# Transposes of two key pairs and their products with the values queued behind each other, the later pair first

## The chip, the cores and the metric

The kernel runs on one core of a Trainium2 chip. A core has a matrix engine (TensorE, PE in the profile; its weight loads are shown apart as PEld), a vector engine (VectorE, DVE), a scalar engine (ScalarE, ACT), a general engine (GpSimd, POOL) and a queue engine that issues the transfers here (SyncE, SP). The metric is device time in microseconds. The time before is a median of 3044.38 us over three runs, 3041.36 to 3046.33.

## What is computed

One layer on a sequence of 2048 rows of width 1024, in float32. A normalised input is projected once; the projection feeds three branches (attention with forget gates, a state-space layer, and attention into 256 memory rows), each is gated, projected back and merged, and an output projection with a residual and a norm closes it. The change is in the first branch, 12 heads of width 64:

```python
def block(args):
    qi, Fi, s0 = args
    s = jnp.einsum('bhqd,bhkd->bhqk', qi, kh)
    s = s + Fi[..., None] - F[:, :, None, :]
    qpos = s0 + jnp.arange(Q_BLOCK, dtype=jnp.int32)
    s = jnp.where(key_pos[None, :] <= qpos[:, None], s, NEG)
    p = jax.nn.softmax(s, axis=-1)
    return jnp.einsum('bhqk,bhkd->bhqd', p, vh)
```

The attention is causal: a query sees the keys up to its own position.

## The kernel before

**Precision.** Matmuls run on operands split into a high and a low part (hi, lo). The transposes take plain float32. The values `v` hold 64 high and 64 low columns side by side, and the transposed probabilities hold 256 high and 256 low columns side by side, so one product of 128 x 512 gives the cross terms; they are added up at the end of a block.

**Stages.** First the projections, with the state-space layer, the gated unit and the memory attention woven in; then the attention stage; then what is left of the filling, the merge and the output projection (`merge_out`). For the attention stage the eight PSUM banks are shared out anew: three for scores (`psA`), three for transposes (`psB`), one for the accumulated output (`psC`), one for the filling (`psF`).

**A block.** A block is a head `h` and a group `G` of 256 queries (0 to 7), held as two tiles `P[1]` and `P[0]` of 128 queries each; a group sees 2G+2 tiles of 128 keys, taken as G+1 key pairs `kp`. `fox_scores` computes for each of the two query tiles the scores on PE (L751, L752, pieces of up to 512 keys), adds the forget term and takes the maximum on DVE (L753), the exponential on ACT (L758) and the division on POOL (L762). `fox_pv` (L766) then takes one key pair at a time:

- four transposes of 128 x 128 into one `psB` bank (L783; three at the diagonal, where the first query tile does not see the last key tile);
- a cast of the bank to the high half of a `Pt` tile on ACT (L786), and the remainder into the low half on DVE (L787); at the diagonal in two pieces each (L791, L792). There are three `Pt` buffers;
- two products with the values (L799), which accumulate over all key pairs in the block's one `psC` bank.

Behind the last pair the bank is added up (`ot`, L802 and L803), multiplied by a gate and stored (L805 to L808).

**The order.** `gen_fox` (L810) is a Python generator that runs through the blocks. While the scores of one block are written down, the key pairs of the block before it are taken between them: half of its steps after the first query tile, the rest after the second. A step is what `fox_pv` does up to a `yield`, one key pair. After each `yield` of `gen_fox`, `run` adds 0.355 (`PACE`) to a due count, and whenever that reaches 1 it lets the filling go one step: the rest of the projection of the merge gates (`gen_gl`), then the merge of the last quarter (`gen_merge0`), six matmuls or so a step on `psF`. A step of the filling is queued on PE behind the product that was the last one written down 8 yields earlier (`LAG`, kept in `self.pe` and `marks`).

The order of the text isn't the order of issue. A scheduler goes through the program with simulated durations; on each engine it issues what is ready, by priority, which is the order of the text. An engine's issued order is then fixed, and each engine works through its own in turn. `issue_after(x)` puts the instructions of its block that are on the engine of `x` behind `x`; `high_priority()` lets an instruction go ahead of others that are ready.

The rest of the names: `hd` holds a head's keys, values and forget terms; `po` is the `psC` bank; `load_w` (L134) and `split` (L888) bring weights and split them on POOL (L893) or ACT (L891) and DVE (L895); `mm3` (L144) issues three matmuls for a split product (L147 to L149).

Of the kernel before, what the change touches and what calls it, by code (L numbers as in the profile page):

```python
# [5 lines left out]
F32R = mybir.dt.float32r  # L6
# [39 lines left out]
def fl32(ap):  # L46
    return ap.bitcast(F32)


class Layer:  # L50
# [649 lines left out]
        close()  # L700


    def open_fox(self):
        self.fp, self.close_fp = self.pool("foxh", side="right")
        self.k0, self.q0 = [self.fox_keys(0, 0), self.fox_keys(0, 1)], self.fox_q(0, 3)
# [60 lines left out]
    def fox_pv(self, p, h, hd, G, P):  # L766

        nc, s = self.nc, self.s
        po = self.psC()
        cs = slice(G * 256, (G + 1) * 256)  # L770
        r = slice(h * DH, (h + 1) * DH)
        gf = p.tile([64, 256], F32, tag="gf", name="gf", bufs=2)
        nc.sync.dma_start(out=gf, in_=s["gf"][r, cs])
        for kp in range(G + 1):
            ps = self.psB()
            t = p.tile([128, 2, 512], F32R, tag="Pt", name="Pt", bufs=3)
            hi, lo = t[:, :, 0:256], t[:, :, 256:512]
            for a in range(2):
                kt = 2 * kp + a
                for b in range(2):  # L780
                    if kt <= 2 * G + b:
                        o = a * 256 + b * 128
                        nc.tensor.transpose(ps[:, o:o + 128], P[b][:, kt * 128:(kt + 1) * 128], self.ident)  # L783
            psv = ps.rearrange("p (a n) -> p a n", a=2)
            if kp < G:
                nc.scalar.copy(hi, psv)  # L786
                nc.vector.tensor_sub(lo, psv, fl32(hi))  # L787
            else:
                for a in range(2):
                    c = slice(a * 128, 256)  # L790
                    nc.scalar.copy(hi[:, a, c], psv[:, a, c])  # L791
                    nc.vector.tensor_sub(lo[:, a, c], psv[:, a, c], fl32(hi[:, a, c]))  # L792
            for a in range(2):
                kt = 2 * kp + a
                v = hd[kt // 8][1][:, kt % 8, :]
                o, m = po, t[:, a, :]
                if kt == 2 * G + 1:
                    o, m = (z.rearrange("p (x b n) -> p x b n", x=2, b=2)[:, :, 1, :] for z in (o, m))
                self.pe = nc.tensor.matmul(o, v, m, start=(kt == 0), stop=(kt == 2 * G + 1))  # L799
            yield  # L800
        t = p.tile([128, 256], F32, tag="ot", name="ot", bufs=1)
        nc.scalar.copy(t, po[:, 256:512])  # L802
        nc.vector.tensor_add(t, po[:, 0:256], t)  # L803
        o = p.tile([64, 256], F32, tag="oo", name="oo", bufs=2)
        nc.scalar.copy(o, t[64:128])  # L805
        nc.gpsimd.tensor_add(o, o, t[0:64])
        nc.gpsimd.tensor_mul(o, o, gf)
        nc.sync.dma_start(out=s["yx"][r, cs], in_=o)  # L808
# [352 lines left out]
```

## Time and profile before

| what | value |
| --- | --- |
| median of three runs | 3044.38 us (3041.36 to 3046.33) |
| the profiled execution | 3032.29 us, of it 3030.5 us from the first to the last instruction |
| granted clock of TensorE over the span | 0.992 |
| transposes L783 | 1632 |
| products L799 | 864 |
| casts L786 and L791 | 336 and 192 |
| subtractions L787 and L792 | 336 and 192 |

The profile is one execution of the program. Times are in microseconds from the span's start. Matmuls overlap each other, so the duration that a row gives for one is longer than its distance to the next; distances from start to start tell what it costs in a stream. A row of the waits has who waited, for whom, the sum, the times and the longest. A row of the groups has the line, the engine, the operation, the tiles, the form and the count, then busy time and the mean of one in nanoseconds, then the idle time ahead of them and what ended it. In the timeline and in the chain a row has the start, the length and the instructions, neighbours of one kind merged.

### The profile page before, as it was taken

How to read it: one execution, taken by the hardware profiler on the slowest of the kernel's cores; microseconds unless marked ns; L12 is line 12 of the kernel's file. 1: busy time of each engine (PE TensorE's matmuls, PEld its weight loads, DVE VectorE, ACT ScalarE, POOL GpSimd, SP SyncE). 2: the span in 40 equal slices, each digit the busy share in tenths (PEclk: the TensorE clock that was granted, in tenths of full speed). 3: DMA queues.
4: the chain of work that ended last, by engine and by line, in shares of the span. 5: the costliest groups of instructions: out<-in, count | busy, mean ns of one | idle time of the engine just before them, and what ended most of it. 6: DMA issues, size and time to landing. Idle time of an engine off the chain costs nothing.

```text
span 3030.5 us, 43647 instructions
## 1 busy us (share of the span) xinstructions
PE 2956.7 (98%) x14656; PEld 2424.2 (80%) x14656; DVE 1842.2 (61%) x4982; ACT 1044.1 (34%) x2049; POOL 864.8 (29%) x1160
## 2 busy tenths in 40 slices
PE   9999999999999999999999999999999897999999
PEld 7889977777777778888878888888888786788787
DVE  5333399899896673322216777777777875554444
ACT  5102111111112231222215666666666563332222
POOL 0010000000002342112215665565665662222100
PEclk9999999999999999999999999999999999999999
DMA  5343323323334655344352433444443548776542
GB/s 169 108 126 107 106 87 106 126 87 116 122 130 150 175 167 172 105 135 132 116 167 87 123 116 112 117 119 118 126 119 114 172 123 264 226 244 209 175 146 98
DMA packets 306671, 417.80 MB, mean 138 GB/s; under 512 B 84084, under 2 KB 165236, under 8 KB 306436
## 3 DMA queue, kind: packets, MB, share of 16 engines
q1 hardware_dynamic: 306160, 414.95, 44.9%
q8 instruction: 116, 1.90, 0.3%
q14 instruction: 107, 0.88, 0.1%
q10 hardware_dynamic: 288, 0.07, 0.0%
HBM read 276.00 MB, written 138.90 MB: 137 GB/s over the span
## 4 chain that ended last, share of the span: by engine, by line
PE 80%; DMA 9%; DVE 5%; issue 3%; POOL 2%; ACT 1%; SPq 0%; DVEq 0%; POOLq 0%; ACTq 0%
PE psF L147 10%; PE psF L148 10%; PE psF L149 10%; PE psA L149 8%; PE psA L147 8%; PE psA L148 8%; PE psC L799 6%; PE psB L783 5%; PE psA L752 3%; PE psA L751 3%; PE psC L147 2%; PE psC L149 2%; PE psC L148 2%; DMA wraw<-in_w_out 1%; DMA yr<-s_ys 1%
## 5 line engine op out<-in xcount | busy, mean ns | idle before, releaser
L147 PE MATMUL psF<-hh,whi 128*128 128x512 f32 (+1 forms) x1160 | 468.2, 404 | 5.5 <-DVE elo L228 2.5
L149 PE MATMUL psF<-hh,wlo 128*128 128x512 f32 (+1 forms) x1160 | 459.5, 396 | 0.0
L148 PE MATMUL psF<-hl,whi 128*128 128x512 f32 (+1 forms) x1160 | 459.1, 396 | 0.0
L893 POOL TENSOR_SCALAR whi<-wraw 128x1024 fp32r<-128x1024 f32 (+2 forms) x134 | 137.0, 1023 | 710.3 <-PE psA L148 307.0
L147 PE MATMUL psA<-hh,whi 128*128 128x512 f32 (+1 forms) x816 | 322.6, 397 | 2.5 <-POOL whi L893 1.5
L148 PE MATMUL psA<-hl,whi 128*128 128x512 f32 (+1 forms) x816 | 323.9, 397 | 0.0
L149 PE MATMUL psA<-hh,wlo 128*128 128x512 f32 (+1 forms) x816 | 321.8, 395 | 0.8 <-DVE wlo L895 0.8
L895 DVE TENSOR_TENSOR wlo<-wraw,whi 128x1024 fp32r<-128x1024 f32 (+2 forms) x168 | 204.9, 1221 | 191.8 <-POOL whi L893 152.5
L799 PE MATMUL psC<-Pt,v 128*128 128x512 f32 x864 | 266.1, 398 | 6.8 <-DVE ot L803 3.4
L787 DVE TENSOR_TENSOR Pt<-psB,Pt 128x512 fp32r<-128x512 f32 x336 | 226.4, 686 | 75.7 <-ACT Pt L786 73.2
L147 PEld LDWEIGHTS psF<-hh,whi 128*128 128x128 f32 x1160 | 218.6, 188 | 52.2 <-DVE elo L228 3.2
L149 PEld LDWEIGHTS psF<-hh,wlo 128*128 128x128 f32 x1160 | 218.4, 188 | 51.3 <-DVE wlo L895 0.4
L148 PEld LDWEIGHTS psF<-hl,whi 128*128 128x128 f32 x1160 | 218.7, 189 | 45.7 <-issue 0.4
L753 DVE CUSTOM_DVE_ANT_0 P<-psA,nf 128x512 f32<-128x512 f32 (+1 forms) x336 | 201.3, 627 | 45.7 <-PE psA L752 25.4
L786 ACT CAST Pt<-psB 128x512 fp32r<-128x512 f32 x336 | 191.7, 585 | 97.3 <-PE psB L783 52.4
L762 POOL TENSOR_SCALAR P<-P,rd 128x768 f32<-128x768 f32 (+1 forms) x240 | 192.1, 815 | 61.5 <-DVE rd L759 40.6
L751 PE MATMUL psA<-kk,qh 128*128 128x512 f32 (+1 forms) x480 | 185.1, 391 | 3.4 <-DVE mx L753 1.6
L147 PEld LDWEIGHTS psA<-hh,whi 128*128 128x128 f32 x816 | 154.0, 189 | 38.0 <-POOL whi L893 1.9
L149 PEld LDWEIGHTS psA<-hh,wlo 128*128 128x128 f32 x816 | 154.4, 189 | 35.9 <-DVE wlo L895 1.2
L148 PEld LDWEIGHTS psA<-hl,whi 128*128 128x128 f32 x816 | 154.4, 189 | 33.4
L799 PEld LDWEIGHTS psC<-Pt,v 128*128 128x128 f32 x864 | 153.8, 190 | 33.7 <-DVE Pt L787 5.6
L783 PE MATMUL psB<-ident,P 128*128 128x128 f32 x1200 | 176.3, 273 | 0.3
(373 smaller groups left out, 6243.1 us busy)
## 6 DMA issues: line engine op xcount, KB each, us to landing
wraw<-in_w_in SPq DMA_DIRECT2D x90, 512.0 KB, 4.1
s_gl<-ehi SPq DMA_DIRECT2D x96, 256.0 KB, 2.6
g<-s_gl SPq DMA_DIRECT2D x96, 256.0 KB, 4.6
wraw<-in_w_proj SPq DMA_DIRECT2D x40, 320.0 KB, 4.0
s_vs<-ev_v SPq DMA_DIRECT2D x48, 256.0 KB, 2.7
nf<-s_nf SPq DMA_DIRECT2D x24, 512.0 KB, 6.6
v<-s_vs SPq DMA_DIRECT2D x24, 512.0 KB, 6.1
qh<-s_qh SPq DMA_DIRECT2D x96, 128.0 KB, 3.7
```

Of the source, the lines that this page charges most:

```text
L147: nc.tensor.matmul(out, a[0], b[0], start=first, stop=False)
L148: nc.tensor.matmul(out, a[0], b[1], start=False, stop=False)
L149: nc.tensor.matmul(out, a[1], b[0], start=False, stop=last)
L751: nc.tensor.matmul(ps[:, :wm], q[0][:, qs], kk[:, c0:c0 + wm], start=True, stop=False)
L753: nc.vector.tensor_tensor_reduce(out=pr[:, c * 512:c * 512 + w], in0=ps[:, :w], in1=nf[:, c0:c0 + w], scale=1.0, scalar=-3.0e38, op0=ALU.a ...
L762: nc.gpsimd.tensor_scalar(out=c, in0=c, scalar1=rd, scalar2=0.5, op0=ALU.mult, op1=ALU.mult)
L783: nc.tensor.transpose(ps[:, o:o + 128], P[b][:, kt * 128:(kt + 1) * 128], self.ident)
L786: nc.scalar.copy(hi, psv)
L787: nc.vector.tensor_sub(lo, psv, fl32(hi))
L799: self.pe = nc.tensor.matmul(o, v, m, start=(kt == 0), stop=(kt == 2 * G + 1))
L893: self.nc.gpsimd.tensor_scalar(out=hi, in0=x, scalar1=sc, scalar2=1.0, op0=ALU.mult, op1=ALU.mult)
L895: self.nc.vector.tensor_sub(lo, x, fl32(hi))
```

## The change

`fox_pv` takes two key pairs at a time, `j` and `j + 1` (the last one alone where G+1 is odd). It takes two `psB` banks and two `Pt` tiles, and writes down the transposes of both pairs, the later pair's first. Each transpose but the first is put behind the one before it (`issue_after`) and given high priority, by the new helper `behind`. The casts and subtractions follow, the earlier pair's first. Where there are two pairs, a `yield` stands here. Then come the products, four of them, again the later pair's first and each behind the one before it. Since the order of the accumulation has changed, the flag that starts it goes with the first product written down and the flag that ends it with the last. The number of yields of a block stays at G+1.

```diff
@@ -1,3 +1,5 @@
+from contextlib import contextmanager
+
 import concourse.bass as bass
 import concourse.tile as tile
 from concourse import mybir
@@ -700,6 +702,15 @@
         close()
 
 
+    @contextmanager
+    def behind(self, last):
+
+        if last is None:
+            yield
+        else:
+            with self.tc.issue_after(last.ins), self.tc.high_priority():
+                yield
+
     def open_fox(self):
         self.fp, self.close_fp = self.pool("foxh", side="right")
         self.k0, self.q0 = [self.fox_keys(0, 0), self.fox_keys(0, 1)], self.fox_q(0, 3)
@@ -771,32 +782,45 @@
         r = slice(h * DH, (h + 1) * DH)
         gf = p.tile([64, 256], F32, tag="gf", name="gf", bufs=2)
         nc.sync.dma_start(out=gf, in_=s["gf"][r, cs])
-        for kp in range(G + 1):
-            ps = self.psB()
-            t = p.tile([128, 2, 512], F32R, tag="Pt", name="Pt", bufs=3)
-            hi, lo = t[:, :, 0:256], t[:, :, 256:512]
-            for a in range(2):
-                kt = 2 * kp + a
-                for b in range(2):
-                    if kt <= 2 * G + b:
-                        o = a * 256 + b * 128
-                        nc.tensor.transpose(ps[:, o:o + 128], P[b][:, kt * 128:(kt + 1) * 128], self.ident)
-            psv = ps.rearrange("p (a n) -> p a n", a=2)
-            if kp < G:
-                nc.scalar.copy(hi, psv)
-                nc.vector.tensor_sub(lo, psv, fl32(hi))
-            else:
+        first = True
+        for j in range(0, G + 1, 2):
+            kps = range(j, min(j + 2, G + 1))
+            pss = {kp: self.psB() for kp in kps}
+            ts = {kp: p.tile([128, 2, 512], F32R, tag="Pt", name="Pt", bufs=3) for kp in kps}
+            last = None
+            for kp in reversed(kps):
                 for a in range(2):
-                    c = slice(a * 128, 256)
-                    nc.scalar.copy(hi[:, a, c], psv[:, a, c])
-                    nc.vector.tensor_sub(lo[:, a, c], psv[:, a, c], fl32(hi[:, a, c]))
-            for a in range(2):
-                kt = 2 * kp + a
-                v = hd[kt // 8][1][:, kt % 8, :]
-                o, m = po, t[:, a, :]
-                if kt == 2 * G + 1:
-                    o, m = (z.rearrange("p (x b n) -> p x b n", x=2, b=2)[:, :, 1, :] for z in (o, m))
-                self.pe = nc.tensor.matmul(o, v, m, start=(kt == 0), stop=(kt == 2 * G + 1))
+                    kt = 2 * kp + a
+                    for b in range(2):
+                        if kt <= 2 * G + b:
+                            o = a * 256 + b * 128
+                            with self.behind(last):
+                                last = nc.tensor.transpose(pss[kp][:, o:o + 128], P[b][:, kt * 128:(kt + 1) * 128], self.ident)
+            for kp in kps:
+                t = ts[kp]
+                hi, lo = t[:, :, 0:256], t[:, :, 256:512]
+                psv = pss[kp].rearrange("p (a n) -> p a n", a=2)
+                if kp < G:
+                    nc.scalar.copy(hi, psv)
+                    nc.vector.tensor_sub(lo, psv, fl32(hi))
+                else:
+                    for a in range(2):
+                        c = slice(a * 128, 256)
+                        nc.scalar.copy(hi[:, a, c], psv[:, a, c])
+                        nc.vector.tensor_sub(lo[:, a, c], psv[:, a, c], fl32(hi[:, a, c]))
+            if j + 1 <= G:
+                yield
+            last = None
+            for kp in reversed(kps):
+                for a in range(2):
+                    kt = 2 * kp + a
+                    v = hd[kt // 8][1][:, kt % 8, :]
+                    o, m = po, ts[kp][:, a, :]
+                    if kt == 2 * G + 1:
+                        o, m = (z.rearrange("p (x b n) -> p x b n", x=2, b=2)[:, :, 1, :] for z in (o, m))
+                    with self.behind(last):
+                        self.pe = last = nc.tensor.matmul(o, v, m, start=first, stop=(j + 2 > G and kp == j and a == 1))
+                    first = False
             yield
         t = p.tile([128, 256], F32, tag="ot", name="ot", bufs=1)
         nc.scalar.copy(t, po[:, 256:512])
```

## The prediction

> **What bounds the kernel now.** I read the page first, then the busy times by stretch, then the waits, then the chain and the timeline inside the stage that the change touches.
>
> ```profile
> span 3030.5 us, 43647 instructions
> PE 2956.7 (98%) x14656; PEld 2424.2 (80%) x14656; DVE 1842.2 (61%) x4982; ACT 1044.1 (34%) x2049; POOL 864.8 (29%) x1160
> PE 80%; DMA 9%; DVE 5%; issue 3%; POOL 2%; ACT 1%; SPq 0%; DVEq 0%; POOLq 0%; ACTq 0%
> ```
>
> TensorE (PE) is busy 98% of the span and holds 80% of the chain that ended last. The transposes (L783) and the products with the values (L799) run only in the attention stage, about 1605 to 2520 us. Its stretches (columns: length; busy us and count of PE, PEld, DVE, ACT, POOL; granted clock; DMA share; GB/s):
>
> ```profile
> 1605.00:2520.00 915.00, 898.82 (x4830) 747.67 (x4830) 680.14 (x2023) 575.41 (x1161) 559.71 (x794) 0.99 0.42 123
> 1605.00:2340.00 735.00, 729.15 (x3967) 609.63 (x3967) 538.09 (x1659) 476.49 (x954) 439.96 (x636) 1.00 0.40 115
> 2340.00:2520.00 180.00, 169.66 (x866) 138.03 (x865) 142.05 (x365) 98.92 (x208) 119.75 (x158) 0.97 0.52 154
> ```
>
> In 915.0 us PE stands idle for 16.2 us: 5.9 us in the first 735 us (0.8%), 10.3 us in the last 180 us. DVE is busy 74%, ACT 63%. So the stage has two parts that the change can move: the PE time of the instructions themselves, and these 16.2 us. The waits of PE in the stage that name the edited lines:
>
> ```profile
> PE psC L799 <- DVE ot L803: 3.4, 1, 3.4
> PE psC L799 <- DVE Pt L787: 2.9, 2, 2.6
> PE psC L799 <- DVE Pt L792: 0.2, 1, 0.2
> ACT Pt L786 <- PE psC L799: 39.7, 46, 3.3
> ```
>
> Out of 864 products, 4 made PE wait, for 6.5 us in all. The last row is the other direction: ACT waited 46 times for a product to give back a `Pt` buffer, so the ring of three `Pt` buffers is already used up at times, with PE not suffering from it.
>
> **What the change costs, part by part.**
>
> *Number of instructions.* The same transposes, casts, subtractions and products are issued, the same buffers are declared, and no DMA is added, removed or moved past another: the load of `gf` stays in the first step of a block, the store of `yx` behind the last. A block has G+1 steps before and after, so the pace of the filling work (0.355 of a step for each) is the same. The sum is therefore over order alone. Blocks G = 0 to 7 give 0, 1, 1, 2, 2, 3, 3, 4 groups of two, 16 a head, 192 in 12 heads; 48 single key pairs are left.
>
> *Transposes in longer runs.* A run of 4 becomes a run of 8, or of 7 at the diagonal. Does a change between transposes and other matmuls cost something that a longer run saves? The chain view shows runs of all these lengths as they stand (start, us, what):
>
> ```profile
> 1975.00 0.33 PE psB L783 x3
> 1980.40 0.44 PE psB L783 x4
> 1981.30 0.44 PE psB L783 x4
> 1652.76 0.76 PE psB L783 x7
> 1995.16 0.87 PE psB L783 x8
> 2069.24 1.31 PE psB L783 x12
> ```
>
> 3 take 0.33 us, 4 take 0.44, 7 take 0.76, 8 take 0.87, 12 take 1.31: 0.11 us each at every length. The matmul that follows a run might hide a cost, so I check from start to start in the timeline:
>
> ```profile
> 1901.82 1.55 PE L799 MATMUL psC<-Pt,v 128*128 128x512 f32 x6
> 1903.21 0.60 PE L783 MATMUL psB<-ident,P 128*128 128x128 f32 x4
> 1903.57 0.48 PE L147 MATMUL psF<-hh,whi 128*128 128x512 f32 x1
> 1903.89 0.40 PE L148 MATMUL psF<-hl,whi 128*128 128x512 f32 x1
> ...
> 2154.12 1.04 PE L783 MATMUL psB<-ident,P 128*128 128x128 f32 x8
> 2154.92 0.48 PE L751 MATMUL psA<-kk,qh 128*128 128x512 f32 x1
> 2155.23 0.40 PE L752 MATMUL psA<-kk,ql 128*128 128x512 f32 x1
> ```
>
> Six products start 1901.82 and are replaced at 1903.21, 0.23 us each. From the first of 4 transposes to the second matmul behind them is 1903.89 - 1903.21 = 0.68 us; less one matmul of 0.23 that is 0.45 us. For 8 it is 2155.23 - 2154.12 = 1.11, less 0.23, 0.88 us. Two runs of 4 cost 0.90 or 0.88 us, one of 8 costs 0.88 or 0.87: between nothing and 0.02 us less. The price of a change of kind is zero to within the rounding; over 192 groups that bounds the gain at about 4 us, and by the equal runs of 3 to 12 I take **0**.
>
> *Products in fours.* Products in a run cost 0.23 us each, as single matmuls of the filling do (1903.89 above stands 0.32 behind 1903.57 only because that one follows transposes, and this is in the sum just made). **0**.
>
> *The added wait.* The first product of a group is now the later pair's, and the earlier pair's follow it in order: PE must have both casts and both subtractions before all four are through. Behind a waiting product PE's queue holds the other three, and then filling matmuls and scores; for them wait the casts that need a free `Pt`, and on ACT behind those the exponentials. The rows for one pair:
>
> ```profile
> L787 DVE TENSOR_TENSOR Pt<-psB,Pt 128x512 fp32r<-128x512 f32 x336 | 226.4, 686 | 75.7 <-ACT Pt L786 73.2
> L786 ACT CAST Pt<-psB 128x512 fp32r<-128x512 f32 x336 | 191.7, 585 | 97.3 <-PE psB L783 52.4 <-PE psC L799 39.7 <-DVE mx L753 2.2
> L895 DVE TENSOR_TENSOR wlo<-wraw,whi 128x1024 fp32r<-128x1024 f32 (+2 forms) x42 | 58.8, 1400 | 7.5 <-POOL whi L893 5.1 <-ACT whi L891 2.3
> ```
>
> One cast more and one subtraction more is at most 0.585 + 0.686 = 1.27 us; with no cover at all, 192 x 1.27 = 244 us, the far upper bound. Cover is there: 432 pairs in 915 us give PE 2.12 us of work for a pair, 4.24 for a group. The ring sets the tightest loop: with three `Pt` buffers and two in a group, the next group's second cast starts only when the last group's products are done. Products 4 x 0.23 = 0.93, cast 0.59, subtraction 0.69: 2.2 us of the 4.24, which leaves 2.0 us for what stands ahead on ACT and DVE. The usual neighbour on DVE is shorter than that (1.40 us in the mean for the longest kind). So I keep the three waits on `Pt` that exist and make each longer by one subtraction: 3 x 0.69 = **+2 us**. Below, the wait can only shrink by what is there: 6.5 us, and the cold clock behind it.
>
> *Buffers given back earlier.* The second pair's transposes no longer stand behind the first pair's products, so `P` comes free a step sooner; DVE waited for that, but PE did not, so **0**. In return two of the three `psB` banks are taken at once; the next group's first pair has one bank, its second waits for a subtraction that is due before the products anyway: **0** unless the ring binds.
>
> A rule of the Trainium skill, "TensorE: Matmul & The Clock Gate", Part 4, speaks against longer runs: it says that transposes do not count as TensorE activity for the clock gate in the way matmuls do. What it would do here is priced under the rivals; the stretch to 2340 us ran at a granted clock of 1.00 with runs of 8 and 12 in it, so the trace so far speaks against it.
>
> Sum: 0 + 0 + 2 + 0 = +2 us. The profiled execution took 3032.3 us for its span of 3030.5; the median of the runs is 3044.4 (3041.4 to 3046.3), 0.4% above it. Since what I add is a difference, I put it on the median: **3046 us**.
>
> **The rivals.** A measurement of this kernel can tell about 0.2%, 6 us, from no change.
>
> *Faster: stalls go.* The biggest single stall of a product is the 3.4 us for `ot`, the one accumulator bank handed from block to block. Now the first step of a block holds only transposes, so its first product comes later and `ot` has had time. Idle time of PE is also paid for afterwards:
>
> ```profile
> 2355.24 0.50 PE L147 MATMUL psF<-ymg,whi 128*128 128x512 f32 x1 [2.29 <-POOL ymg L893]
> ...
> 2356.05 0.63 PE L751 MATMUL psA<-kk,qh 128*128 128x512 f32 x1
> 2356.48 0.63 PE L752 MATMUL psA<-kk,ql 128*128 128x512 f32 x1
> ...
> 2358.83 0.63 PE L147 MATMUL psF<-ymg,whi 128*128 128x512 f32 x1
> 2359.25 0.69 PE L783 MATMUL psB<-ident,P 128*128 128x128 f32 x4
> ```
>
> After 2.29 us of idling matmuls stand 0.43 apart instead of 0.23; the timeline shows that from 2356.05 to 2359.25, eight of them, 8 x 0.20 = 1.6 us. All 6.5 us of the products' waits with one such tail give 8 us less: 3036 us. The far bound is all 16.2 us with three tails (5 us): 3023. For it: every wait named is at a point that the change moves. Against it: with 4 waits in 864 the old order was hardly late.
>
> *Slower: the ring of `Pt`.* The 2.0 us of margin are gone when something long stands ahead of a cast or a subtraction. It happens now:
>
> ```profile
> 1865.88 3.07 DVE L895 TENSOR_TENSOR wlo<-wraw,whi 128x1024 fp32r<-128x1024 f32 x1
> ...
> 1869.01 1.26 DVE L787 TENSOR_TENSOR Pt<-psB,Pt 128x512 fp32r<-128x512 f32 x2
> 1869.73 0.73 PE L799 MATMUL psC<-Pt,v 128*128 128x512 f32 x2 [2.56 <-DVE Pt L787]
> ```
>
> A weight subtraction of 3.07 us held two `Pt` subtractions back, and PE stood 2.56 us. There are 42 such subtractions in the stage, and 2 waits of that kind now. If one in four lands in a group without margin, that is 9 stalls more, 9 x 2.56 = 23 us, and 3067 us; with a tail of 1.6 us on half of them, 3074. It decides from three stalls more (8 us). For it: the 46 waits of ACT for `Pt`, with a ring that has now to serve two at a time. Against it: the filling matmuls may run ahead by 8 steps and are there to stand between.
>
> *The order does not become what the text says.* Chained instructions issue behind each other, but others can come between where a bank or an operand is late; then the runs stay short. By the transposes' rows that costs and brings nothing: 3044 us, inside the forecast's range.
>
> *Slower: the clock.* If a run of 8 (0.87 us) let the clock drop as the idle of 2.29 us did, each would cost the 1.6 us above, 192 x 1.6 = 307 us, 3352 us. The run of 12 stands in a stretch at clock 1.00, so this is nearly out. That is what the skill's rule would make of it.
>
> **How the numbers follow.** No change within 0.2% (my forecast, with the order that does not form): 0.42, own range 3038 to 3051. Stalls go: 0.24. The ring: 0.32. The clock: 0.02. Faster 0.24, same 0.42, slower 0.34. For 8 in 10 the range leaves out the deep end of the gain (all idle time gone) and the ring's cost beyond the nine stalls with their tails, and the clock: **3030 to 3076 us**.
>
> **What would show it.** Right: runs of 8 and 7 of L783 at 0.87 and 0.76 us, runs of 4 of L799 at 0.93, PE idle in the stage still near 16 us, clock 1.00 up to the filling's change. The ring: the wait of L799 for `Pt` L787 grows from 2.9 us to over 10, and ACT's wait for L799 well over 39.7. The gain: the row of L799 on `ot` is gone and nothing has come for it. The forecast is wrong in its base if 8 transposes take another time than 0.87 us, or if the end of the attention stage moves against its start by more than PE's idle time does.

## The result, and the profile after

The changed kernel takes 3081.3 us in the median of four runs (3076.9 to 3083.5), the kernel before, run beside it, 3044.7. The ratio is 1.0119, with a 95% interval of 1.0107 to 1.0132: 36.6 us slower, and 5 us above the end of the range. The two profiled executions stand 50.1 us apart (3032.3 and 3082.4); that of before is on the low side of its runs. I use the traces for where the time went and the ratios for how much.

The first and last start of the products with the values show where. From the view of that line, before and after (the first number group is the shortest, middle and longest duration in ns):

```profile
L799 PE MATMUL psC<-Pt,v x864: 274/393/775, 1612.1 to 2513.4; 128*128 128x512 f32 x154, 128*128 128x256 f32 x19
```

```profile
L822 PE MATMUL psC<-Pt,v x864: 274/395/775, 1616.1 to 2566.8; 128*128 128x512 f32 x156, 128*128 128x256 f32 x17
```

901.3 us became 950.7: the attention stage alone grew by 49.4 us, nearly all of the 50.1. What the stage computes is unchanged, so the time is waiting. Three rows of before that are wanted below come first: PE's wait at the scores, and two waits of the casts at the diagonal. Behind them stand the busy times of the changed kernel in the stretch that was quoted of before, and in its whole stage the waits of PE and large ones of all engines:

```profile
PE psA L751 <- DVE mx L753: 1.6, 3, 0.7
ACT Pt L791 <- PE psB L783: 36.7, 40, 2.9
ACT Pt L791 <- DVE Pt L792: 26.9, 31, 3.9
```

```profile
1605.00:2340.00 735.00, 710.86 (x3768) 578.51 (x3766) 510.14 (x1567) 450.35 (x901) 417.12 (x602) 1.00 0.38 109
```

```profile
PE psA L762 <- DVE mx L764: 12.9, 8, 5.6
PE psB L798 <- DVE Pt L805: 9.6, 17, 1.6
...
PE psC L822 <- DVE ot L827: 2.6, 2, 2.2
PE psC L822 <- DVE Pt L805: 2.3, 2, 1.7
```

```profile
POOL nf L750 <- DVE mx L764: 190.1, 76, 9.0
DVE Pt L805 <- ACT Pt L804: 99.6, 122, 4.2
ACT Pt L804 <- PE psB L798: 95.2, 75, 4.8
ACT Pt L809 <- DVE Pt L810: 80.5, 56, 3.2
...
ACT Pt L804 <- PE psC L822: 46.6, 59, 2.1
...
ACT Pt L809 <- PE psB L798: 2.6, 10, 0.9
```

PE idles 24.1 us in the 735 us, where it idled 5.9. Short stalls are not in that number: a matmul's modelled duration of 0.4 us covers a stall of up to 0.16. That matters here. From 1605 us to the end of the stage (2520 us before, 2570 now) PE idles 42.8 us instead of 16.2, which is 26.6 of the 49.4; the rest stands as busy time, 922.2 us instead of 898.8 for the same instructions. The products themselves wait for `Pt` hardly differently, 2.3 us against 2.9 (and 1.0 against 0.2 at the diagonal). What grew is in front of them. The casts of full pairs on ACT (L804) wait for transposes 95.2 us instead of 52.4. The casts at the diagonal (L809) wait for transposes less, 2.6 instead of 36.7, but for subtractions 80.5 instead of 26.9. These are the second pieces of a diagonal tile, which wait for the subtraction of the tile's first piece; this wait on ACT grew most. The subtractions on DVE wait for casts 99.6 instead of 73.2; PE now waits for DVE at the scores (12.9 us, 1.6 before) and at the transposes (9.6 us, none listed before). Each engine works through its queue in the issued order, and the queues have fallen out of step. One group in the changed kernel's timeline shows how:

```profile
2043.91 0.60 PE L798 MATMUL psB<-ident,P 128*128 128x128 f32 x4
...
2047.12 0.60 PE L798 MATMUL psB<-ident,P 128*128 128x128 f32 x4
...
2047.76 0.59 ACT L804 CAST Pt<-psB 128x512 fp32r<-128x512 f32 x1 [2.00 <-PE psB L798]
2048.24 2.01 ACT L769 ACTIVATE P<-P,nm 128x2048 f32<-128x2048 f32 x1
2048.38 0.69 DVE L805 TENSOR_TENSOR Pt<-psB,Pt 128x512 fp32r<-128x512 f32 x1
...
2050.24 0.57 ACT L804 CAST Pt<-psB 128x512 fp32r<-128x512 f32 x1
...
2051.50 0.69 DVE L805 TENSOR_TENSOR Pt<-psB,Pt 128x512 fp32r<-128x512 f32 x1
```

By the issued orders with their buffer numbers, the first four transposes are the later pair's, the next four the earlier pair's, and the two casts are the earlier pair's and then the later one's. So the later pair's bank is full at 2044.5 and nobody empties it. ACT's queue has the earlier pair's cast first, whose transposes come only at 2047.12: ACT idles 2.00 us. The later pair's cast follows at 2050.24 behind an exponential, its subtraction ends at 2052.2, and one of three `psB` banks has been held 8.3 us.

A count in the issued orders: of the transposes in the stage, 237 runs of 4 and 40 of 8 (271 and 19 before); of the products, 147 runs of 4 (48 before). The products did come mostly in fours. Most transposes did not come in eights.

### The profile page after: what moved, and what is told of

It reads as the page before. It is cut to its first block, busy times and chain, and to the rows that moved or that the text cites. A ratio compares the mean times of both kernels' runs of the same rounds, so it can differ in the third digit from the quotient of the medians.

```text
span 3080.6 us, 43423 instructions
## 1 busy us (share of the span) xinstructions
PE 2982.2 (97%) x14656; PEld 2421.8 (79%) x14656; DVE 1842.7 (60%) x4982; ACT 1043.4 (34%) x2049; POOL 864.9 (28%) x1160
## 4 chain that ended last, share of the span: by engine, by line
PE 74%; DMA 11%; DVE 6%; issue 3%; POOL 3%; ACT 2%; SPq 1%; DVEq 0%; POOLq 0%; ACTq 0%
PE psF L149 9%; PE psF L150 9%; PE psF L151 9%; PE psA L151 8%; PE psA L149 8%; PE psA L150 7%; PE psC L822 4%; PE psB L798 4%; PE psA L762 2%; PE psA L763 2%; DMA nf<-s_nf 2%; PE psC L149 2%; PE psC L151 2%; PE psC L150 2%; DMA s_mg<-g 1%
## 5 line engine op out<-in xcount | busy, mean ns | idle before, releaser
L805 DVE TENSOR_TENSOR Pt<-psB,Pt 128x512 fp32r<-128x512 f32 x336 | 225.9, 685 | 100.8 <-ACT Pt L804 99.6
L822 PE MATMUL psC<-Pt,v 128*128 128x512 f32 x864 | 250.6, 400 | 6.7 <-DVE ot L827 2.6
L804 ACT CAST Pt<-psB 128x512 fp32r<-128x512 f32 x336 | 190.0, 585 | 146.1 <-PE psB L798 95.2
L762 PE MATMUL psA<-kk,qh 128*128 128x512 f32 (+1 forms) x480 | 188.3, 395 | 18.1 <-DVE mx L764 12.9
L798 PEld LDWEIGHTS psB<-ident,P 128*128 128x128 f32 x1200 | 146.4, 141 | 39.6 <-DVE Pt L805 8.1
```

The source lines that it names most:

```text
L762: nc.tensor.matmul(ps[:, :wm], q[0][:, qs], kk[:, c0:c0 + wm], start=True, stop=False)
L798: last = nc.tensor.transpose(pss[kp][:, o:o + 128], P[b][:, kt * 128:(kt + 1) * 128], self.ident)
L822: self.pe = last = nc.tensor.matmul(o, v, m, start=first, stop=(j + 2 > G and kp == j and a == 1))
```

## The experiments

Theories: **R**, the ring of three `Pt` buffers binds because a group holds two. **B**, the three `psB` banks bind because a group takes two. **W**, the products wait for two casts and two subtractions whatever the buffers. Later **O** (the order with the later pair first costs), and out of it **M** (it costs where transposes, casts and products disagree) against **L** (the later pair first costs by itself). Every ratio is to the kernel before, run on the same chip beside it.

### Buffers and banks

The changed kernel with fewer `Ps` buffers, and with their space given to a fourth `Pt`:

```diff
-PB, PBS = 4, 4
+PB, PBS = 4, 3
```

> The changed kernel with three instead of four of the short probability buffers Ps. It is the control for the next run, which needs their space. Both theories: within 10 us of the changed kernel's 3081, since TensorE's waits name psA, psB and Pt and none names Ps.

Ratio 1.0194 (1.0171 to 1.0216), 3095.7 us. Missed: that buffer did cost, 0.75 points over the changed kernel, though PE's waits had named it only once, for 0.3 us.

```diff
-            ts = {kp: p.tile([128, 2, 512], F32R, tag="Pt", name="Pt", bufs=3) for kp in kps}
+            ts = {kp: p.tile([128, 2, 512], F32R, tag="Pt", name="Pt", bufs=4) for kp in kps}
```

> As the control, with four Pt buffers instead of three, so that a second group can be cast in full before the first one's products are done. Ring of Pt (theory R): most of the loss comes back, 3055 us or less, and ACT's wait for L822 falls below 15 us. Banks (theory B: the earlier pair's transposes wait for the second psB bank): within 8 us of the control, since psB stays at three. Lateness (theory W: the products wait for two casts and two subtractions whatever the buffers): within 8 us of the control.

Ratio 1.0163 (1.0135 to 1.0192), 3088.3 us, 7 us under its control, which is not clear of the noise. R as I had it falls. Its sign came: the casts' wait for L822 went from 32.4 us in the control to 2.1. The time did not come with it: the fourth buffer brings a small part at most, and the casts now wait 125.3 us for transposes, where the control has 106.7:

```profile
ACT Pt L804 <- PE psB L798: 125.3, 106, 4.3
```

Then one bank from the scores to the transposes, in the changed kernel and in the kernel before:

```diff
-PS2 = {"A": 3, "B": 3, "C": 1, "F": 1}
+PS2 = {"A": 2, "B": 4, "C": 1, "F": 1}
```

> The changed kernel with four psB banks and two psA banks in the attention stage. Theory B: the transposes of both pairs find a bank each, TensorE's wait for psB (9.6 us in the changed kernel) falls under 2 us, and against the next run, which has the same banks in the kernel before, less than 12 us remain. R and W: 30 us or more remain against the next run.

> The kernel before with four psB and two psA banks: the control for the run above. Every theory leaves it open; two psA banks make the scores wait for DVE, so 3050 to 3110 us.

1.0099 (1.0079 to 1.0119), 3067.0 us, and 1.0108 (1.0087 to 1.0128), 3068.9 us: the same, as B had it and not as R and W had it. With the fourth bank the casts of the changed kernel no longer wait for transposes; they wait for a product to give back `Pt`. The first two rows are the changed kernel's, the other two its control's:

```profile
ACT Pt L804 <- PE psB L798: 3.2, 4, 2.0
ACT Pt L804 <- PE psC L822: 125.0, 92, 5.8
```

```profile
ACT Pt L786 <- PE psB L783: 16.2, 17, 2.7
ACT Pt L786 <- PE psC L799: 85.3, 98, 3.0
```

The wait for transposes is 3.2 us against 95.2 in the change, that for `Pt` 125.0 against 46.6: most of the waiting moved one place on. PE's wait for `psB` fell only to 5.5 us, where B had less than 2. The size can't be read from this pair, since two score banks slow the control by 32 us and may hide the rest. So it says that the change's waits for transposes go through the banks, and neither why the banks are held nor that they are the cost.

### Which order costs

In the next four both pairs are written down together, with two banks and two `Pt` tiles and the same yields. Only the order and the chains differ. The plain version:

```diff
-            for kp in reversed(kps):
+            for kp in kps:
...
-                            with self.behind(last):
+                            with self.behind(None):
                                 last = nc.tensor.transpose(pss[kp][:, o:o + 128], P[b][:, kt * 128:(kt + 1) * 128], self.ident)
...
-            for kp in reversed(kps):
+            for kp in kps:
...
-                    with self.behind(last):
-                        self.pe = last = nc.tensor.matmul(o, v, m, start=first, stop=(j + 2 > G and kp == j and a == 1))
+                    with self.behind(None):
+                        self.pe = last = nc.tensor.matmul(o, v, m, start=first, stop=(j + 2 > G and kp == kps[-1] and a == 1))
```

> The two pairs are written down together, earlier pair first in both parts, nothing queued behind anything. Theory B in its strict form (two banks taken at once is the cost) and theory R (two Pt held at once): the loss stays, ratio to the kernel before 1.008 or more. Theory O (order: what costs is that the later pair goes first, because each bank and each buffer of the group is then held until the other pair is done): the scheduler is free to start as before, ratio within 0.998 to 1.003.

Ratio 0.9991 (0.9980 to 1.0002). Writing both pairs down together, with two banks and two buffers asked for at once, costs nothing. B and R in their strict form are out, and O stands.

With the chains and the priority kept, only `reversed` gone from both loops:

> The changed kernel with the chains and the priority kept, but the earlier pair first in transposes and products. O: most of the loss is gone, ratio 1.000 to 1.005. B and R: the loss stays, 1.008 or more. If the priority or the chains are the cost: it stays too, and the plain version is free of it.

Ratio 0.9999 (0.9990 to 1.0008). The chains and the priority cost nothing either.

With `reversed` and the chain in the transposes alone, the products as in the plain version:

> Transposes later pair first and chained; products earlier pair first, free. O: a part of the loss, ratio 1.003 to 1.009: casts still come in the order of the text, so the earlier pair's cast waits for the transposes that now come last, but the products of a pair can start alone. If products alone carry it: within 0.998 to 1.003.

Ratio 1.0059 (1.0044 to 1.0074). And in the products alone, the transposes as in the plain version:

> Transposes earlier pair first, free; products later pair first and chained, so each product waits for both pairs' casts and subtractions. O with the late products as its main part: ratio 1.006 to 1.012, TensorE's waits on psA and psB as in the changed kernel. If the transposes alone carry it: within 0.998 to 1.003.

Ratio 1.0064 (1.0047 to 1.0081). Of the waits expected, that on `psA` came (10.6 us, 12.9 in the change), that on `psB` did not (2.0 us, 9.6 in the change). Each half costs about 0.6%, and both together 1.2%. They wait for different things. The casts' waits with the transposes turned, and with the products turned:

```profile
ACT Pt L804 <- PE psB L798: 102.4, 91, 3.1
DVE Pt L805 <- ACT Pt L804: 98.0, 120, 3.0
ACT Pt L804 <- PE psC L822: 18.2, 27, 2.0
```

```profile
ACT Pt L804 <- PE psC L822: 111.5, 99, 3.7
DVE Pt L805 <- ACT Pt L804: 87.8, 126, 3.6
ACT Pt L804 <- PE psB L798: 20.9, 50, 1.1
```

With the transposes turned the casts wait mostly for transposes; with the products turned, mostly for a product to give back `Pt`. The second is no measure of the loss, as the next run shows.

### Is it the later pair, or the disagreement?

In the changed kernel the casts and subtractions kept the text's order, the earlier pair first. Turning them as well:

```diff
-            for kp in kps:
+            for kp in reversed(kps):
                 t = ts[kp]
                 hi, lo = t[:, :, 0:256], t[:, :, 256:512]
```

> The changed kernel with the casts and subtractions in the later pair's order too, so that transposes, casts and products agree again. Theory M (what costs is that the three orders disagree: a cast in the text's order waits for the transposes issued last, and a product issued first waits for the subtraction issued last): the loss goes, ratio 0.999 to 1.004. Theory L (the later pair going first costs by itself): the loss stays, 1.009 or more.

Ratio 0.9971 (0.9959 to 0.9982), 3028.3 us, a little below M's range. One line takes the whole loss away, with the transposes and products still later pair first and chained. L falls. PE's busy time in the first 735 us is that of the kernel before again, and the casts' wait for transposes is below it (52.4). Their wait for `Pt` is not: 92.5 us, twice that of the change, and no loss:

```profile
ACT Pt L804 <- PE psB L798: 36.5, 36, 2.7
ACT Pt L804 <- PE psC L822: 92.5, 93, 3.1
```

```profile
1605.00:2340.00 735.00, 729.28 (x3955) 607.93 (x3954) 533.74 (x1655) 477.63 (x951) 441.16 (x636) 1.00 0.41 115
```

With this edit, but the products earlier pair first and free, so that only they disagree:

> Transposes, casts and subtractions later pair first; products earlier pair first. The transposes and casts agree, the products disagree with both, the mirror of the run with the products alone reversed. M: ratio 1.004 to 1.010, as there. If only products that go later pair first cost: 0.998 to 1.003.

Ratio 1.0058 (1.0043 to 1.0073): the mirror of the turned products, at the same price.

The changed kernel without the priority:

```diff
-            with self.tc.issue_after(last.ins), self.tc.high_priority():
+            with self.tc.issue_after(last.ins):
```

> The changed kernel with the chains but without the high priority. M: the orders still disagree, ratio 1.009 to 1.014. If the priority takes issue slots from scores and filling and so is a cost of its own: 1.006 or less.

Ratio 1.0125 (1.0102 to 1.0149): the loss stays.

Last, the plain version with nothing but the casts and subtractions turned:

> Transposes and products earlier pair first and free, as in the plain version; only the casts and subtractions later pair first. Nothing on TensorE is written in another order than before. M: both agreements are broken, as in the changed kernel, ratio 1.009 to 1.014. If the loss needs TensorE's own order to be turned: 0.998 to 1.003.

Ratio 1.0107 (1.0090 to 1.0124). PE's text has the earlier pair first here, as before, and the loss is there in full.

Together (E is the earlier pair first, L the later one):

| transposes | casts | products | disagreements | ratio |
| --- | --- | --- | --- | --- |
| E | E | E (plain; chained) | 0 | 0.9991; 0.9999 |
| L | L | L | 0 | 0.9971 |
| L | E | E | 1, at the banks | 1.0059 |
| E | E | L | 1, at `Pt` | 1.0064 |
| L | L | E | 1, at `Pt` | 1.0058 |
| L | E | L (the change; no priority) | 2 | 1.0119; 1.0125 |
| E | L | E | 2 | 1.0107 |

In the issued orders too, all 192 groups of each of these runs stand as the table has them. The price is about 0.6% for each place where two neighbours in the chain disagree, wherever the later pair stands. I followed each numbered buffer through the traces. The means are in us over the 432 banks and their `Pt` tiles: from the last transpose (counted as 0.11 us) to the bank's first cast, from the first transpose to the end of the last subtraction, and from that end to the tile's first product:

```
                     last transpose to its cast   bank held   subtraction to its product
before                         1.56                  4.13              2.67
transposes turned              2.21                  4.78              2.22
products turned                2.15                  4.57              3.16
the change                     2.42                  4.96              2.23
only the casts turned          2.46                  4.96              1.93
all turned                     1.51                  4.07              2.73
```

In the kernel before and with all turned, a full bank waits about 1.5 us for its cast and is held 4.1 us; in the change 2.4 and 5.0. With the products turned it is held longer too, 4.6 us, though transposes and casts agree there. The products' turn shows in the last column, 3.2 us against 2.7, but not in the change, where both places disagree.

Which waits go with the loss? In us over the stage, 1605 to 2570, the casts of L804 and L809 taken together:

| | casts for transposes | casts for `Pt` | second piece at the diagonal | subtractions (L805) for casts | PE at the scores (L762) for DVE |
| --- | --- | --- | --- | --- | --- |
| before | 89.1 | 42.3 | 26.9 | 73.2 | 1.6 |
| plain | 77.7 | 53.2 | 30.7 | 71.2 | 4.1 |
| earlier first, chained | 53.3 | 85.7 | 23.0 | 74.2 | 4.0 |
| all turned | 60.5 | 92.5 | 35.8 | 64.6 | 4.3 |
| transposes turned | 118.0 | 21.9 | 55.3 | 98.0 | 13.3 |
| products turned | 22.9 | 158.0 | 38.1 | 87.8 | 10.6 |
| all but the products turned | 9.6 | 150.9 | 57.8 | 90.9 | 14.1 |
| the change | 97.8 | 56.5 | 80.5 | 99.6 | 12.9 |
| only the casts turned | 122.2 | 32.0 | 61.1 | 103.8 | 9.6 |

The first two columns say where the casts wait, not whether it costs: the change waits little more for transposes than the kernel before. The last two part the four versions without loss clearly from the five with it, and the one before them just does. DVE waits for ACT, ACT at the diagonal waits for DVE, and PE waits for DVE to empty a score bank. That the disagreement costs is shown by the ratios; this way from it to PE is read from the waits, and no run took one of them away alone. Theory W survives in part: a product that needs the subtraction that comes last is the second of the two places.

## Why the prediction was wrong

- *What bounds the kernel.* Right: PE was nearly full, 5.9 us idle in 735, and the change could only move order and waiting.
- *Transposes in longer runs, products in fours: 0.* Right. Where eight transposes do come in a run, they take what was read from the trace of before (the chain view of the changed kernel):

```profile
1664.78 0.88 PE psB L798 x8
1670.07 0.87 PE psB L798 x8
```

- *The added wait: +2 us.* **This step failed.** It kept the three waits of products for `Pt` and made "each longer by one subtraction". Those waits hardly changed, 3.1 us before and 3.3 after, and the loss of 36.6 us arose elsewhere: two disagreements of order at about 0.6%, 18 us, each, with casts and subtractions waiting for each other and PE waiting at the score banks. I had named the new text order of transposes and products and had not set it beside the order of the casts, which the change leaves earlier pair first. In ACT's queue, a cast whose transposes come last then holds up the one whose bank is full (2.00 us in the group shown), and PE's first product of a group needs the subtraction that comes last. The cover I counted, 2.0 us of margin in a mean group, was a mean; the group shown above needed 8.3 us from transposes to a free bank, where the mean was 4.24 us for a group.
- *Buffers given back earlier; two of three `psB` banks at once: 0 "unless the ring binds".* Half right. Asking for two at once costs nothing (0.9991). With the orders of the change a bank is held 0.8 us longer in the mean; how much of the loss that is by itself stays open.
- *The rival of the ring, 3067 to 3074 us, 0.32.* Right sign, too small, and its own sign did not come: the wait of L822 for `Pt` did not pass 10 us, and a fourth `Pt` won 7 of the control's 59 us, within the noise. When the products alone are turned, casts wait 111.5 us for `Pt`, but with all turned they wait 92.5 and nothing is lost. Whether a fourth buffer would cure the first case was not tried.
- *The rival of the stalls that go.* The wait for `ot` did shrink, from 3.4 to 2.6 us, and is no measure of the whole. The tail of 1.6 us that it counted was a little high: two of the eight matmuls have 384 columns and stand 0.32 us apart, which makes about 1.5.
- *The order does not become what the text says: 3044 us.* It half did not: most transposes stayed in fours. In the group above the second bank came free at 2045.1 us, and filling and score matmuls stand between the two fours. But a run that is broken up is not the old order, and it cost.
- *The clock.* Out: granted 1.00 in the stretch to 2340 us, in both kernels. The Trainium skill ("TensorE: Matmul & The Clock Gate", Part 4) has transposes not counting as activity in the same way; runs of 8 and 12 transposes between matmuls did not lower the clock here.

The version with all three turned is the fastest of the runs, 0.29% under the kernel before. In the two profiled executions, which differ by 4.8 us where the medians differ by 10, the gain isn't in the attention stage:

```profile
L822 PE MATMUL psC<-Pt,v x864: 274/395/682, 1613.3 to 2516.7; 128*128 128x512 f32 x156, 128*128 128x256 f32 x17
```

That is 903.4 us against 901.3. From 2520 to 3020 us PE is busy 478.3 us instead of 473.9 (before first, then all turned), nearly the whole difference:

```profile
2520.00:3020.00 500.00, 473.89 (x2003) 379.55 (x2003) 248.78 (x401) 136.05 (x234) 88.64 (x55) 0.98 0.62 198
```

```profile
2520.00:3020.00 500.00, 478.34 (x2022) 380.58 (x2020) 247.15 (x406) 137.60 (x237) 93.41 (x57) 0.99 0.63 198
```

One wait of 8.0 us where the merge begins is in the trace of before, and none like it in this one:

```profile
PE psA L147 <- ACT whi L891: 8.0, 1, 8.0
```

It is for a weight that ACT splits. Why it went was not tested. My guess is how the filling fell at the end of the stage, not the order of the pairs.

## What to carry to other kernels

When a step on one engine is turned round, turn its consumers and their consumers with it: this kernel, whose engines take their queues in a fixed order, paid 0.6% of the whole for each pair of neighbours that disagreed. Such a loss need not show as a wait at the edited instruction. Here it stood engines further on, between casts and subtractions and at the score banks. A large wait by itself says little: look for the ones that go with the time over several versions. And a margin worked out from a mean group says little about a loop of several queues that must stay in step.
